# Feed-forwards' last matrices: the last pair of tiles keeps its seven operands on chip and goes second

## The chip, the cores and the metric

The kernel runs on one core of a Trainium2 chip. The core has a matrix engine (TensorE, PE in the profile), a vector engine (VectorE, DVE), an activation engine (ScalarE, ACT), GpSimd (POOL), and an engine that issues most of the transfers (SyncE, SP). Data lies in HBM, in the on-chip buffer SBUF, and in PSUM, into which TensorE writes its products. SP, ACT and POOL can each start transfers (DMAs); the queue of SP is called SPq in the profile, that of ACT is ACTq. Each engine works through its own list in the order written there, so an instruction that waits holds up everything behind it on that engine.

The metric is the time of one execution on the device in microseconds (us). The kernel before takes 2007.23 us, the median of three runs (2004.85 to 2007.33).

## The reference

One layer of a streaming encoder on 1,040 tokens (16 meta tokens and 1,024 frames) of width 1,024:

```python
h = h + 0.5 * swiglu(rmsnorm(h, ffn1_norm), ffn1_w_gate, ffn1_w_up, ffn1_w_down)
u = rmsnorm(h, mix_norm)
...                                   # window attention and gated linear attention on u @ w_in
h = h + mixed @ w_out
h = h + 0.5 * swiglu(rmsnorm(h, ffn2_norm), ffn2_w_gate, ffn2_w_up, ffn2_w_down)
return rmsnorm(h, final_norm)[:, N_META:]

def swiglu(x, w_gate, w_up, w_down):
    return (silu(x @ w_gate) * (x @ w_up)) @ w_down
```

The change concerns the two feed-forwards (`ffn1`, `ffn2`). The inner width is 2,816, which is 22 tiles of 128 columns. All of it is 32-bit: each factor of a product is split into a high and a low part, and three products of the parts are added.

## The kernel before, in words

**A feed-forward in two halves.** The class `Seven` holds one feed-forward. In the first half, `gate_up(f)` makes one tile f of the inner activations, silu(gate) times up, transposed: 128 inner columns by all tokens, as two halves m0 and m1 of the tokens (520 tokens each in the first feed-forward, 512 in the second). In the second half, `down`, the inner activations are multiplied with `w_down` and added to h.

**Seven products instead of eight.** Both halves use a 2 by 2 block scheme with seven products (`PRODUCTS`), each a sum of a weight block times a sum of activation blocks. The seven right-hand operands are called B11, B21, T2, T1, T3, B22 and T4. For `down` they are made from a pair of tiles, f = 2p and 2p + 1. `middle(f, m0, m1)` collects two tiles and appends seven little pieces of work to the list `pending`; `pump` does the next of them whenever it is called, which is seven times in each `gate_up` and at seven slots at the beginning of `down`. Such a piece subtracts blocks where the operand is a difference (VectorE, L277) and then calls `keep`: high part by ScalarE (L237), low part by VectorE (L238), two transfers into a tensor `mid` in HBM (L240, L241).

**The second half.** `down` runs over five groups of two pairs (`NG` = 5), each group in two steps, one for each half of the output columns, so ten steps of seven slots. A slot is one of the seven products: 24 matmuls of 260 columns in the first feed-forward, 12 of 512 in the second. In slot i TensorE multiplies the weight operand `w` (made two slots ahead by ScalarE L228 and VectorE L229, the tiles `wop`) with the operand `tm` of both pairs. The 14 operand tiles of the first group are loaded by SP before the first slot. Those of the next groups are loaded through ACT's own queue, one per slot, in the order in which they are needed (`load_t`, L347). When a slot's sum is complete it goes from PSUM to h: the first time by ScalarE (L396), afterwards by VectorE (`add_half`, L341). GpSimd makes the four sums of weight blocks for the next step (L437). From the second step on the old h is read back (`old`, L408) and added (L404).

**The last pair.** The pair of tiles 18 and 19 is finished when `down` begins. Its seven pieces of work, in `down`'s first slots, use four small buffers (`ttile`), and their transfers go through GpSimd, since `ending` is set. The pair is loaded again with its partner as the fifth and last group.

**The two tiles outside the groups.** 22 tiles are five groups of four and two left over (`LAST` = 2, tiles 20 and 21). These go to `w_down` as plain products at the very end (`load_last`), and their high and low parts are kept in `last_dram`. Some tiles are computed before the scheme starts, as plain products. In the first feed-forward these are tiles 20 and 21 (`HEADS`) and tile 0; in the second they are tiles 0 and 1 (`heads`), and tiles 2 to 21 run through `gate_ups`.

**What sets the order.** A scheduler orders each engine's instructions from the program's text, its data and its buffers. An operand buffer `tm` comes from one of two rings: eight buffers for B11 and B21 and twenty for the others, which is what two groups need. During the first half the same buffers hold the activation operands (`tt`, `tb`).

## Time and profile before

| | us |
|---|---|
| median of three runs | 2007.23 |
| the profiled execution | 2007.16 |
| span in its profile | 2005.5 |
| TensorE busy in the span | 1979.6 |
| VectorE, ScalarE, GpSimd busy | 1406.9, 895.9, 178.5 |
| first feed-forward's `down`, from its first product | 480.10 on |
| second feed-forward's `down`, from its first product | 1772.68 on |

The span goes from the first to the last instruction that the profiler recorded. Times within it are in us from its start. A row of the timeline of one engine gives start, duration, engine, line, operation and how many like it follow each other; in square brackets it gives the idle time just before, and what ended it. A row of busy time by stretches gives the stretch, its length, then busy time and number of instructions of PE, PEld (weight loads), DVE, ACT and POOL, then the granted clock of TensorE as a share of full speed, the busy share of the 16 DMA engines and GB/s. A row of transfers gives what is written from what, the queue, the count, the size in KB of 1,024 bytes and the median time in us from issue to landing.

### The profile page before, as it was taken

To read this page: it belongs to the slowest core of one execution; us is meant where nothing else is said; L and a number is where in the kernel's file an instruction comes from. 1 tells how busy PE (TensorE), PEld (TensorE's weight loads), DVE (VectorE), ACT (ScalarE), POOL (GpSimd) and SP (SyncE) were. 2 spreads that over 40 slices of the span, in tenths; PEclk is the share of its full clock that TensorE was granted. 3 is DMA by queue.
4 is the path that set the end of the run, shared out by engine and by line. 5 is a ranking of instruction groups with operands and counts; after the bars stand their busy time and mean duration, and the time that the engine had idled before them with its cause. 6 is when DMAs were issued, how large, how long until landed. Compare 5 with 4: busy or idle time off the path is not lost.

```text
span 2005.5 us, 31822 instructions
## 1 busy us (share of the span) xinstructions
PE 1979.6 (99%) x11964; PEld 1756.2 (88%) x11964; DVE 1406.9 (70%) x2455; ACT 895.9 (45%) x1756; POOL 178.5 (9%) x214
## 2 busy tenths in 40 slices
PE   8999999999999999999999999999999999999998
PEld 7999999999999988888888878888888888878887
DVE  6976776676778786476466568469767767757786
ACT  5544444443322254465366545345444444442225
POOL 1000000002323000004100000110000000022220
PEclk9999999999999999999999999999999999999999
DMA  6243453349975333356212647741534534699832
GB/s 212 86 149 128 149 180 129 125 147 378 363 278 199 96 128 106 117 178 180 53 54 69 213 146 224 238 148 47 189 126 148 189 126 140 206 362 346 299 106 85
DMA packets 284619, 343.03 MB, mean 171 GB/s; under 512 B 26407, under 2 KB 192033, under 8 KB 284465
## 3 DMA queue, kind: packets, MB, share of 16 engines
q1 hardware_dynamic: 265376, 274.82, 41.6%
q10 hardware_dynamic: 17296, 61.29, 8.1%
q0 software_dynamic: 1792, 4.89, 0.7%
q8 instruction: 94, 1.54, 0.3%
q14 instruction: 61, 0.49, 0.1%
HBM read 220.66 MB, written 120.27 MB: 170 GB/s over the span
## 4 chain that ended last, share of the span: by engine, by line
PE 92%; DVE 3%; DMA 2%; issue 1%; ACT 1%; POOL 0%; SPq 0%; POOLq 0%; ACTq 0%; DVEq 0%
PE pb L454 36%; PE pd L454 18%; PE pa L454 9%; PE pj L96 2%; PE pj L97 2%; PE pj L98 2%; PE wo L96 1%; PE wo L98 1%; PE wo L97 1%; PE br L96 1%; PE br L98 1%; PE br L97 1%; PE pd L841 1%; PE pj L929 1%; PE pj L930 1%
## 5 line engine op out<-in xcount | busy, mean ns | idle before, releaser
L454 PE MATMUL pb<-tt,wop 128*128 128x260 f32 (+1 forms) x2280 | 393.0, 326 | 0.0
L454 PEld LDWEIGHTS pb<-tt,wop 128*128 128x128 f32 x2280 | 339.7, 188 | 35.5
L228 ACT CAST wop<-s 128x512 fp32r<-128x512 f32 x268 | 166.1, 621 | 235.4 <-PE pb L454 97.4
L229 DVE TENSOR_TENSOR wop<-s,wop 128x512 fp32r<-128x512 f32 x268 | 188.8, 707 | 116.2 <-ACT wop L228 115.7
L454 PE MATMUL pb<-tm,wop 128*128 128x260 f32 (+1 forms) x1440 | 236.4, 320 | 8.0 <-DMA tm<-f2mid 3.5
L454 PEld LDWEIGHTS pb<-tm,wop 128*128 128x128 f32 x1440 | 208.2, 189 | 28.5 <-ACT h L396 2.8
L228 ACT CAST wop<-raw 128x512 fp32r<-128x512 f32 x201 | 124.9, 622 | 221.8 <-PE pb L454 113.2
L229 DVE TENSOR_TENSOR wop<-raw,wop 128x512 fp32r<-128x512 f32 x201 | 144.0, 718 | 30.9 <-ACT wop L228 30.7
L454 PE MATMUL pd<-tt,wop 128*128 128x260 f32 (+1 forms) x792 | 138.2, 327 | 0.0
L454 PEld LDWEIGHTS pd<-tt,wop 128*128 128x128 f32 x792 | 118.8, 188 | 13.1
L341 DVE SCALAR_TENSOR_TENSOR h<-pb,h 128x520 f32<-128x520 f32 (+1 forms) x136 | 93.9, 692 | 39.7 <-PE pb L454 37.7
L454 PE MATMUL pd<-tm,wop 128*128 128x260 f32 (+1 forms) x720 | 118.8, 319 | 0.0
L454 PE MATMUL pb<-tb,wop 128*128 128x260 f32 (+1 forms) x696 | 115.3, 319 | 0.7 <-DVE m L742 0.7
L454 PE MATMUL pd<-tb,wop 128*128 128x260 f32 (+1 forms) x696 | 115.1, 319 | 0.0
L454 PE MATMUL pa<-tb,wop 128*128 128x260 f32 (+1 forms) x696 | 115.0, 318 | 0.0
L454 PEld LDWEIGHTS pd<-tm,wop 128*128 128x128 f32 x720 | 104.3, 188 | 9.3
L454 PEld LDWEIGHTS pb<-tb,wop 128*128 128x128 f32 x696 | 100.9, 188 | 10.1 <-ACT vec L87 0.8
L454 PEld LDWEIGHTS pa<-tb,wop 128*128 128x128 f32 x696 | 100.7, 188 | 9.4
L454 PEld LDWEIGHTS pd<-tb,wop 128*128 128x128 f32 x696 | 100.7, 188 | 9.4
L437 DVE TENSOR_TENSOR s<-raw 128x512 f32<-128x512 f32 x92 | 63.2, 687 | 56.1 <-DMA raw<-in_ffn_w_up 52.8
L96 PE MATMUL pj<-uh,whi 128*128 128x512 f32 (+2 forms) x256 | 91.5, 357 | 0.0
L437 POOL TENSOR_TENSOR s<-raw 128x512 f32<-128x512 f32 x28 | 37.8, 1351 | 595.4 <-DMA raw<-in_ffn_w_down 472.5
(418 smaller groups left out, 3888.0 us busy)
## 6 DMA issues: line engine op xcount, KB each, us to landing
tm<-f1mid ACTq DMA_DIRECT2D x56, 520.0 KB, 6.3
tm<-f2mid ACTq DMA_DIRECT2D x56, 512.0 KB, 5.7
raw<-in_ffn_w_gate SPq DMA_DIRECT2D x42, 512.0 KB, 3.9
raw<-in_ffn_w_up SPq DMA_DIRECT2D x42, 512.0 KB, 4.0
raw<-in_ffn_w_down SPq DMA_DIRECT2D x80, 256.0 KB, 5.3
f2mid<-kh SPq DMA_DIRECT2D x70, 256.0 KB, 2.9
f2mid<-kl SPq DMA_DIRECT2D x70, 256.0 KB, 3.1
f1mid<-kh SPq DMA_DIRECT2D x63, 260.0 KB, 2.7
```

Source lines behind the costliest of these rows:

```text
L96: nc.tensor.matmul(ps, wh[k], xh[k], start=(k == 0), stop=False)
L97: nc.tensor.matmul(ps, wh[k], xl[k], start=False, stop=False)
L98: nc.tensor.matmul(ps, wl[k], xh[k], start=False, stop=(k == n - 1))
L228: nc.scalar.copy(x[:, 0:n], src)
L229: nc.vector.tensor_sub(x[:, n:2 * n], src, x[:, 0:n].bitcast(F32))
L341: nc.vector.scalar_tensor_tensor(hm, ps, 0.5, hm, op0=ALU.mult, op1=ALU.add)
L437: (eng.tensor_add if add else eng.tensor_sub)(a[s], a[x], a[y])
L454: nc.tensor.matmul(ps, y, z[:, s0:s0 + sn], start=(first and k == 0 and at == 0), stop=(at == 2 and k == len(cols) - 1), skip_group_check= ...
L841: nc.tensor.matmul(ps, y, x[:, c0 + s0:c0 + s0 + sn], start=(n == 0), stop=(n == 3 * LAST - 1), skip_group_check=True)
L929: nc.tensor.matmul(ps[:, 0:n], wh, xh, start=(k == 0), stop=False)
L930: nc.tensor.matmul(ps[:, 0:n], wh, xl, start=False, stop=False)
```

## The change

The last pair's operands are no longer written to HBM and read back. `middle` sends the pieces of pair 18, 19 to `halves`, which writes high and low part into an operand buffer `tm` (`down_tile`) that `down` then uses in place. Since these buffers are held until used, the group with this pair goes second: `ORDER` is [0, 4, 1, 2, 3]. The second group loads only its first pair, seven tiles; `load_t` skips the other seven. The branch in `keep` for the end (`ttile`, GpSimd) is gone.

So that the last pair is the last thing that `gate_ups` makes in the second feed-forward too, its plain tiles are now the last two, as in the first: `heads` uses `HEADS` (tiles 20 and 21), and `gate_ups` runs over tiles 0 to 19. Their four `keep`s into `last_dram` happen at the start of the first half instead of at the end.

```diff
+    ORDER = [0, NG - 1, *range(1, NG - 1)]
...
         def keep(self, dst, src):
-            hi, lo = [ttile(x, F32R, self.n) if self.ending else self.block(x, F32R) for x in ("kh", "kl")]
+            hi, lo = [self.block(x, F32R) for x in ("kh", "kl")]
             nc.scalar.copy(hi, src)
             nc.vector.tensor_sub(lo, src, hi.bitcast(F32))
-            eng = nc.gpsimd if self.ending else nc.sync
-            eng.dma_start(out=dst[:, 0:self.n], in_=hi.bitcast(F32))
-            eng.dma_start(out=dst[:, self.n:], in_=lo.bitcast(F32))
+            nc.sync.dma_start(out=dst[:, 0:self.n], in_=hi.bitcast(F32))
+            nc.sync.dma_start(out=dst[:, self.n:], in_=lo.bitcast(F32))
...
-                    self.keep(d[NAMES.index(n)], src)
+                    if f == NF - LAST - 1:
+                        self.here[n] = self.halves(self.down_tile(n), src)
+                    else:
+                        self.keep(d[NAMES.index(n)], src)
...
-        def load_t(self, kg, ts, at, eng):
+        def down_tile(self, n):
+            return self.operand(n in ("B11", "B21"), "tm")
 
-            n, a = NAMES[at // 2], at % 2
-            x = self.operand(n in ("B11", "B21"), "tm")
-            eng.dma_start(out=x.bitcast(F32), in_=self.mid_dram[2 * kg + a, NAMES.index(n)])
-            ts.setdefault(n, []).append(x)
+        def load_t(self, turn, at, eng):
+
+            n, pair = NAMES[at // 2], 2 * ORDER[turn] + at % 2
+            if pair < 2 * NG - 1:
+                x = self.down_tile(n)
+                eng.dma_start(out=x.bitcast(F32), in_=self.mid_dram[pair, NAMES.index(n)])
+                self.ts.setdefault((turn, n), []).append(x)
...
-            kg, half = step // 2, step % 2
+            kg, half = ORDER[step // 2], step % 2
...
-                    pss = [group.product(i, w, ts[step // 2], (j * P, 2 * P + j * P), j, step) for j in range(2)]
+                    ts = {NAMES[i]: self.ts[step // 2, NAMES[i]]}
+                    if step // 2 == 1:
+                        ts[NAMES[i]] = ts[NAMES[i]][0:1] + [self.here[NAMES[i]]]
+                    pss = [group.product(i, w, ts, (j * P, 2 * P + j * P), j, step) for j in range(2)]
...
-    heads = [[ffn2.plain_weights(cols_view(w, f * P)) for w in (ffn2_w_gate, ffn2_w_up)] for f in range(2)]
+    heads = [[ffn2.plain_weights(cols_view(w, f * P)) for w in (ffn2_w_gate, ffn2_w_up)] for f in HEADS]
...
-    for f in range(2):
-        ffn2.middle(f, *out_c[f])
-    ffn2.gate_ups(range(2, NF))
+    for f in range(LAST):
+        ffn2.middle(HEADS[f], *out_c[f])
+    ffn2.gate_ups(range(NF - LAST))
```

The list of TensorE is the same before and after, row for row. The lists of the others differ at the start of both `down`s and at the start of the second feed-forward's first half. Names in the rows: `h` is the output, `wop` a weight operand, `raw` and `s` the weights and their sums, `tm` an operand of `down`, `kh` the high part that `keep` makes. In brackets stand the semaphores that a row waits for: DMAHW0 to DMAHW7 are eight completion semaphores which all transfers of SP and ACT use in turn, DMASW0 to DMASW7 those of GpSimd's transfers. A transfer that takes its turn on DMAHW2 is issued only when the one that used DMAHW2 before it has landed.

ACT, at the beginning of the first feed-forward's `down`, before: four of the second group's loads stand earlier still in the list, and three more stand here between the moves of the first sums from PSUM to h.

```order
L237 CAST kh<-g_5681 128x520 [waits DMASW1_49,DMASW2_49,DMASW0_49,DMASW3_49,DVE_49,Activation_49]
L396 ACTIVATE h_5951<-pb 128x520 [waits PE_49]
L396 ACTIVATE h_5953<-pb 128x520 [waits PE_49]
L228 CAST wop<-raw_5871 128x512 [waits DMAHW7_49]
L347 DMA tm<-f1mid 128x1040 [waits DMAHW4_49]
L347 DMA tm<-f1mid 128x1040 [waits DMAHW6_49]
L228 CAST wop<-raw 128x512 [waits DMAHW0_49,PE_49,Activation_49]
L396 ACTIVATE h_6027<-pb 128x520 [waits PE_49]
L347 DMA tm<-f1mid 128x1040 [waits DMAHW2_49]
L396 ACTIVATE h_6029<-pb 128x520 [waits PE_49]
L396 ACTIVATE h_6067<-pd 128x520 [waits DMAHW0_49,PE_49]
L237 CAST kh<-tm 128x520 [waits DMASW5_49,DVE_49]
```

The same place now:

```order
L229 CAST tm<-g_5681 128x520 [waits DVE_49,Activation_49]
L354 DMA tm<-f1mid 128x1040 [waits DMAHW2_49]
L406 ACTIVATE h_5951<-pb 128x520 [waits PE_49]
L406 ACTIVATE h_5953<-pb 128x520 [waits PE_49]
L229 CAST wop<-raw_5871 128x512 [waits DMAHW3_49]
L354 DMA tm<-f1mid 128x1040 [waits DMAHW5_49]
L229 CAST wop<-raw 128x512 [waits DMAHW4_49,PE_49,Activation_49]
L406 ACTIVATE h_6021<-pb 128x520 [waits PE_49]
L406 ACTIVATE h_6023<-pb 128x520 [waits PE_49]
L229 CAST wop<-raw 128x512 [waits Activation_49]
L229 CAST tm<-tm 128x520 [waits DVE_49]
L406 ACTIVATE h_6058<-pd 128x520 [waits DMAHW4_49,PE_49]
```

The first load of the second group now stands just ahead of the first move to h; none stands between `h_6021` and `h_6023`, the rows that were `h_6027` and `h_6029`. The pieces of the last pair wait for no transfer any more.

ACT, at the beginning of the second feed-forward's `down`, before:

```order
L228 CAST wop<-raw_18333 128x512 [waits DMAHW4_49]
L347 DMA tm<-f2mid 128x1024 [waits DMAHW7_49]
L347 DMA tm<-f2mid 128x1024 [waits DMAHW1_49]
L317 COPY u_18209<-pd 128x512 [waits PE_49]
L228 CAST wop<-s 128x512 [waits Activation_49]
L347 DMA tm<-f2mid 128x1024 [waits DMAHW4_49]
L228 CAST wop<-s 128x512 [waits PE_49,Activation_49]
L347 DMA tm<-f2mid 128x1024 [waits DMAHW7_49]
L228 CAST wop<-s 128x512 [waits PE_49,Activation_49]
L324 ACTIVATE g_18264<-g_18264 128x512 [waits DVE_49]
L228 CAST wop<-s 128x512 [waits PE_49,Activation_49]
```

and now:

```order
L321 COPY u_18150<-pd 128x512 [waits PE_49,Activation_49]
L229 CAST wop<-s 128x512 [waits Activation_49]
L229 CAST wop<-s 128x512 [waits PE_49,Activation_49] x2
L328 ACTIVATE g_18193<-g_18193 128x512 [waits DVE_49]
L229 CAST wop<-s 128x512 [waits PE_49,Activation_49]
L229 CAST tm<-g_18149 128x512 [waits DVE_49]
L354 DMA tm<-f2mid 128x1024 [waits DMAHW6_49,DMAHW4_49]
L406 ACTIVATE h_18335<-pb 128x512 [waits PE_49]
```

The four loads of the second group that stood inside the last `gate_up` are gone from there; the first one follows behind the last `gate_up`'s work.

SP, at the beginning of the first feed-forward's first half, now:

```order
L666 DMA f1last<-kept 128x1040 [waits DMAHW6_49,DVE_49]
L666 DMA f1last<-kept 128x1040 [waits DMAHW7_49,DVE_49]
L418 DMA old<-x_dram 128x520 [waits DMAHW0_49,DVE_49,Activation_49]
L418 DMA old<-x_dram 128x520 [waits DVE_49,DMAHW1_49,Activation_49,Pool_49]
L418 DMA old<-x_dram 128x520 [waits DMASW2_49,DMASW3_49,DMASW1_49,DMAHW2_49,DMASW0_49,PE_49]
L418 DMA old<-x_dram 128x520 [waits DMAHW3_49,DVE_49,Pool_49]
L298 DMA raw<-in_ffn_w_gate 128x8x128 [waits DMAHW4_49,DVE_49]
L298 DMA raw<-in_ffn_w_up 128x8x128 [waits DMAHW5_49,DVE_49]
```

and before:

```order
L656 DMA f1last<-kept 128x1040 [waits DMAHW6_49,DVE_49]
L656 DMA f1last<-kept 128x1040 [waits DMAHW7_49,DVE_49]
L294 DMA raw<-in_ffn_w_gate 128x8x128 [waits DMAHW4_49,DMAHW0_49,DVE_49]
L294 DMA raw<-in_ffn_w_up 128x8x128 [waits DMAHW5_49,DMAHW1_49,DVE_49]
L294 DMA raw<-in_ffn_w_gate 128x8x128 [waits DMAHW0_49,DMAHW2_49,DVE_49,Activation_49]
```

The four `ttile` buffers are no longer used at the end of the first half, so the scheduler has moved the first four reads of the old h to its beginning, ahead of the next weights. In the second feed-forward four such reads stand at the same place.

## The prediction

> **What bounds the kernel now.** I read the page's busy times first, then what TensorE waits for.

> ```profile
> span 2005.5 us, 31822 instructions
> PE 1979.6 (99%) x11964; PEld 1756.2 (88%) x11964; DVE 1406.9 (70%) x2455; ACT 895.9 (45%) x1756; POOL 178.5 (9%) x214
> ```

> ```profile
> PE pb L454 <- DMA tm<-f2mid: 3.5, 2, 2.0
> PE pb L454 <- ACT h L396: 2.6, 1, 2.6
> ...
> PE pb L454 <- DVE h L341: 1.9, 2, 1.3
> ```

> TensorE is idle for 25.9 us in all, and its list of work is the same after the change. So only its gaps can be won. The three rows are all it waits for at L454, 8.0 us, and all lies in the first slots of the two `down`s, where the change acts. I measure what these places cost from start to start of the same product in successive steps, since a stall may also slow what follows. TensorE's timeline, first feed-forward, then the second (`pa` is product 1 of a step):

> ```profile
> 482.96 3.03 PE L454 MATMUL pa<-tm,wop 128*128 128x260 f32 x24
> ...
> 495.85 1.70 PE L454 MATMUL pb<-tm,wop 128*128 128x260 f32 x12 [2.61 <-ACT h L396]
> ...
> 504.58 1.70 PE L454 MATMUL pb<-tm,wop 128*128 128x260 f32 x12 [1.28 <-DVE h L341]
> 506.87 1.71 PE L454 MATMUL pb<-tm,wop 128*128 128x260 f32 x12 [0.60 <-DVE h L341]
> 508.42 3.03 PE L454 MATMUL pa<-tm,wop 128*128 128x260 f32 x24
> ...
> 528.57 1.59 PE L454 MATMUL pa<-tm,wop 128*128 128x260 f32 x12
> ```

> ```profile
> 1775.40 2.88 PE L454 MATMUL pa<-tm,wop 128*128 128x512 f32 x12
> ...
> 1786.28 2.88 PE L454 MATMUL pd<-tm,wop 128*128 128x512 f32 x12
> 1790.68 0.94 PE L454 MATMUL pb<-tm,wop 128*128 128x512 f32 x3 [1.51 <-DMA tm<-f2mid]
> 1793.60 6.69 PE L454 MATMUL pb<-tm,wop 128*128 128x512 f32 x21 [1.98 <-DMA tm<-f2mid]
> 1800.13 2.88 PE L454 MATMUL pa<-tm,wop 128*128 128x512 f32 x12
> ...
> 1819.17 2.88 PE L454 MATMUL pa<-tm,wop 128*128 128x512 f32 x12
> ```

> First feed-forward: the first step takes 508.42 - 482.96 = 25.46 us, the second 528.57 - 508.42 = 20.15. The first loses **5.31 us**, of which 4.49 are gaps. Second: 1800.13 - 1775.40 = 24.73 against 1819.17 - 1800.13 = 19.04, so **5.69 us**, of which only 3.49 are gaps. Most of the rest is in the row of 21 matmuls: 6.69 us, where 12 take 2.72 from start to start (1800.13 is 2.72 before the next product), so 21 should take 4.8. The stretches behind the stall show why:

> ```profile
> 1794.00:1797.00 3.00, 3.00 (x10) 2.32 (x9) 0.51 (x1) 0.00 (x0) 0.00 (x0) 0.58 1.04 384
> 1797.00:1800.00 3.00, 3.00 (x13) 2.41 (x12) 0.00 (x0) 0.16 (x1) 0.88 (x1) 0.85 0.88 302
> 1800.00:1803.00 3.00, 3.00 (x15) 2.49 (x14) 1.50 (x3) 2.93 (x6) 2.92 (x3) 1.00 1.04 303
> ```

> The granted clock falls to 0.58 and 0.85, and at full clock 15 matmuls start where 10 and 13 did. That is 6.69 - 4.8 = 1.9 us which the stall costs beyond its gaps.

> **The change part by part.** *What makes the first stall.* ACT's and VectorE's timelines:

> ```profile
> 494.82 0.33 ACTq L347 DMA_DIRECT2D tm<-f1mid  x1
> 495.19 0.60 ACT L396 ACTIVATE h<-pb 128x520 f32<-128x520 f32 x1 [7.12 <-DMA tm<-f1mid]
> ```

> ```profile
> 503.21 0.70 DVE L238 TENSOR_TENSOR kl<-u,kh 128x520 fp32r<-128x520 f32 x1 [2.32 <-DMA f1mid<-kl]
> ...
> 505.51 0.70 DVE L238 TENSOR_TENSOR kl<-u,kh 128x520 fp32r<-128x520 f32 x1 [0.99 <-DMA f1mid<-kl]
> ```

> ACT could not issue a load of the second group until an earlier transfer had landed; behind it in ACT's list waited the move of a sum to h, and behind that TensorE's next product into the same PSUM (495.85). Then VectorE waited for the small buffers of `keep` to be written out; behind it waited further moves to h (504.58, 506.87). The change removes both: no load stands between these moves any more, and the last pair has no transfer. Term: **-5.31 us**.

> *What makes the second stall.* Operands of the first group arrive late. SP's last ten loads, ACT's first two, and the last of the ten in the chain of waits:

> ```profile
> 1763.08 15.22 SPq L347 DMA_DIRECT2D tm<-f2mid  x10
> ```

> ```profile
> 1762.11 0.81 ACTq L347 DMA_DIRECT2D tm<-f2mid  x2
> ```

> ```profile
> 1777.98 15.58 DMA tm<-f2mid
> ```

> The last load is issued at 1777.98 and lands at 1793.56. Without any stall its first matmul would run 2.72 us (product 5 to 6) and three matmuls of 0.23 after 1786.28, at 1789.7. It must land 3.9 us sooner. The transfers at 1770 to 1795, the sizes and the queues:

> ```profile
> DMA packets 3799, 10.16 MB, mean 407 GB/s; under 512 B 390, under 2 KB 1579, under 8 KB 3797
> ...
> tm<-f2mid ACTq DMA_DIRECT2D x4, 512.0 KB, 7.8
> ...
> f2last<-kh POOLq DMA_DIRECT2D x2, 256.0 KB, 8.7
> ```

> All DMA engines are full and give 0.407 MB per us. What leaves the way of the first group: the eight `f2last` transfers of 0.262 MB (two tiles by two token halves, high and low part; four of them on SP, ahead of these loads, four on GpSimd), 2.1 MB, and the four loads of ACT inside the last `gate_up`, 4 x 0.524 = 2.1 MB. Two of these four vanish with the last pair; the others come later. 4.2 MB at 0.407 are 10.3 us, against 3.9 needed. The first reads of the old h leave this place too. Term: **-5.69 us**. If only part of it comes sooner, a landing still 1 us late costs 1 us.

> *The second group.* Seven loads instead of 14, used from the fifteenth slot on: nothing, and there is nothing to gain, since TensorE waits for nothing there now.

> *What is added.* Seven copies by ScalarE and eleven instructions of VectorE (seven low parts, four differences) in slots 0 to 8 of each `down`. The first feed-forward has them already, as `keep`. In the second, `keep` ran twice, so five copies of some 0.6 us (as ScalarE's row at 495.19) and nine VectorE instructions are new there (the four differences and five low parts). Duration, undisturbed and while GpSimd makes its sums:

> ```profile
> 1758.03 0.69 DVE L238 TENSOR_TENSOR kl<-g,kh 128x512 fp32r<-128x512 f32 x1 [1.49 <-ACT kh L237]
> ...
> 1774.72 1.78 DVE L238 TENSOR_TENSOR kl<-g,kh 128x512 fp32r<-128x512 f32 x1
> ```

> ```profile
> 1772.95 1.30 POOL L437 TENSOR_TENSOR s<-raw 128x512 f32<-128x512 f32 x1 [425.64 <-DMA raw<-in_ffn_w_down]
> ...
> 1777.60 1.74 POOL L437 TENSOR_TENSOR s<-raw,s 128x512 f32<-128x512 f32 x1
> ```

> Slots 0 to 8 last 9 x 2.72 = 24.5 us. VectorE has 9 weight operands, 8 moves to h and these 11 there, 28 x 0.69 = 19.3 us. During GpSimd's four sums, 1772.95 to 1779.34, it does 6.39 / 1.78 = 3.6 instructions where 9.3 would fit, which adds 5.7 x 0.69 = 3.9. That is 23.2 of 24.5 us: hidden, narrowly. Upper bound: GpSimd's next four sums fall into the same slots, 3.9 more, 27.1, which is 2.6 us too much. Nothing can be won here. I take **+0.3 us**, near the lower end, since the first feed-forward does the same work in 25.9 us of slots and stalls on transfers alone, and keep 0 and 2.6.

> *What is moved.* The four `keep`s of the plain tiles go to the start of the second feed-forward, where seven pieces stood; there, near 1400 us, the transfers are far from full (slices 28 and 29 of the page's 40, 47 and 189 GB/s). Nothing.

> ```profile
> GB/s 212 86 149 128 149 180 129 125 147 378 363 278 199 96 128 106 117 178 180 53 54 69 213 146 224 238 148 47 189 126 148 189 126 140 206 362 346 299 106 85
> ```

> The four early reads of the old h stand on SP ahead of the next weights; bounds are under the rivals. I take 0.

> *The sum.* The profiled execution took 2007.16 us, 1.66 more than its span, and agrees with the median of 2007.23. 2007.16 - 5.31 - 5.69 + 0.3 = **1996.5 us**, 0.53% faster.

> **The rivals.** *VectorE becomes the bound.* The sums of GpSimd and the eleven instructions meet, and moves to h come late, as at 504.58. For it: 23.2 of 24.5 us. Against: what the first feed-forward shows. [...] Price: gaps of 1 to 2.6 us, and up to 1.9 for the clock behind them: 1998 to 2001.

> *The low clock stays.* If it had another cause than the gaps, 1.9 us remain: 1998.4. Against: it begins right behind them. [...]

> *The stall only moves.* ACT's loads still wait, in ACT's list, for an earlier transfer to land; the first now stands ahead of the first move to h. If landings are as late as now (15.58 us), ACT is held as at 495.19, and one stall comes back: 1996.5 + 5.3 = 2001.8, or both: 2007. Against: that first load waits for the landing of operands that TensorE needs one slot later anyway, and 4.2 MB are out of the way.

> *Slower: SP is held by the early reads of the old h.* One of the four waits for the buffer that a transposition on TensorE reads, and the weights stand behind it:

> ```profile
> L86 PE MATMUL vps<-ident,vrow x2: 234/252/271, 4.9 to 96.8; 8*128 8x8 f32 x1, 19*128 19x19 f32 x1
> ```

> ```profile
> 100.77 0.38 SPq L294 DMA_DIRECT2D raw<-in_ffn_w_gate  x1
> 103.78 0.38 SPq L294 DMA_DIRECT2D raw<-in_ffn_w_up  x1
> ```

> ```profile
> 115.22 5.75 PE pb L454 x48
> ```

> ```profile
> raw<-in_ffn_w_up SPq DMA_DIRECT2D x42, 512.0 KB, 4.0
> ```

> The weights go out at 100.77 and 103.78 now, and their `gate_up` begins at 118.1 (half of the last row); with 4.0 us of landing and five VectorE instructions of 0.69 (three sums, an operand, one in the way) the slack is 118.1 - 103.8 - 4.0 - 3.4 = 7 us. If a buffer came free only when the running `gate_up` ends, 20.1 us later, each feed-forward would lose 20.1 - 7 = 13 us: 1996.5 + 26 = 2022. It decides when SP is held past about 108 us. Against: as I read the buffers' last uses, that transposition at 96.8 is the latest work that the waits in the list name.

> **How the numbers follow.** Both stalls go: 0.68, 1995 to 1998. The low clock stays: 0.03, 1998.4. VectorE becomes the bound: 0.13, 1998 to 2001. A stall stays or moves: 0.12, 2001.5 to 2007. SP is held: 0.04, above 2007. The range of 1994.5 to 2001.5 leaves out the last two and reaches 2 us below the sum, because runs differ by 2.5 us. A measurement tells 0.2%, 4 us, from no change: faster means below 2003.2. From the third case a third lies there: 0.68 + 0.03 + 0.13 + 0.04 = 0.88; same 0.08; slower 0.04.

> **What would show it.** Right: in TensorE's waits no row for L454 with `tm<-f2mid`, `h L396` or `h L341` above 0.5 us; `pa` to `pa` 20.1 and 19.0 us in the first step too; a granted clock of 1.00 throughout 1770 to 1800; the first group's last load landed before its slot; TensorE's busy time lower by 5.31 + 5.69 - 4.49 - 3.49 = 3 us, the part of the two losses that was no gap. Wrong: a new row for L454 released by VectorE (second case), by ACT or a transfer (third), or a gap at L454 in the first `gate_up`s near 118 or 1410 (fourth).

## The result, and the profile after

The changed kernel takes **1996.19 us** (median of four runs, 1995.26 to 1997.96), the kernel before 2007.28 us beside it (2004.85 to 2009.59). The ratio is 0.9947 with a 95% interval of 0.9933 to 0.9961: 10.6 us less by the ratio (7.8 to 13.4), 11.1 by the medians. The forecast was 1996.5 us and 10.7 us less. The profiled execution took 1996.54 us. The first lines of its page:

```profile
span 1994.6 us, 31746 instructions
PE 1976.3 (99%) x11964; PEld 1755.8 (88%) x11964; DVE 1402.4 (70%) x2455; ACT 897.2 (45%) x1756; POOL 166.9 (8%) x196
```

The span is 10.9 us shorter. TensorE's busy time fell from 1979.6 to 1976.3, its idle time from 25.9 to 18.3: 3.3 us and 7.6 us. The changed kernel's waits of TensorE begin with these rows (in total, times, longest); line 464 is what was line 454.

```profile
PE xps L567 <- DMA x<-in_x: 2.8, 1, 2.8
...
PE pb L464 <- DVE m L752: 0.7, 1, 0.7
```

The only wait left at the products is the 0.7 us at the start of the first half, which stood there before. `tm<-f2mid`, `h L396` and `h L341` are gone. TensorE's timeline where the two `down`s begin:

```profile
482.61 3.03 PE L464 MATMUL pa<-tm,wop 128*128 128x260 f32 x24
...
497.03 5.90 PE L464 MATMUL pb<-tm,wop 128*128 128x260 f32 x48
502.76 3.03 PE L464 MATMUL pa<-tm,wop 128*128 128x260 f32 x24
```

```profile
1770.32 2.88 PE L464 MATMUL pa<-tm,wop 128*128 128x512 f32 x12
...
1789.36 2.88 PE L464 MATMUL pa<-tm,wop 128*128 128x512 f32 x12
```

From `pa` to `pa` the first steps now take 502.76 - 482.61 = 20.15 us and 1789.36 - 1770.32 = 19.04 us, like the steps behind them, where they took 25.46 and 24.73. That is 5.31 + 5.69 = 11.0 us, where the span fell by 10.9 and the profiled execution by 10.6. Outside these two steps the two profiled executions nearly agree: the changed kernel's is 0.35 us shorter ahead of the first `down`, 0.58 longer between the end of that `down`'s first step and the beginning of the second `down`, and 0.13 shorter behind. The stretches in which the clock had been low (columns as before: length, busy time of PE, PEld, DVE, ACT, POOL, granted clock, share of the DMA engines, GB/s):

```profile
1776.00:1779.00 3.00, 3.00 (x15) 2.49 (x14) 1.70 (x4) 3.00 (x7) 0.00 (x0) 1.00 0.55 175
...
1794.00:1797.00 3.00, 3.00 (x15) 2.49 (x14) 0.69 (x1) 1.94 (x4) 0.00 (x0) 1.00 0.83 280
```

The clock is 1.00 throughout, and from 1776 on the DMA engines are no longer full. The operands of the first group, in the rows on SP's loads of `tm` from 1740 to 1800 (instructions, first and last start; then the shortest, median and longest time to landing):

```profile
L354 SPq DMA_DIRECT2D tm<-f2mid x14: 319/351/1217, 1749.4 to 1764.7; - x14
DMA to landing us min/median/max: 4.1/8.4/10.2
```

The last load goes out at 1764.7 and has landed by 1774.9, which is 7.3 us after the `down`'s first product (1767.60). Before, it landed 1793.56 - 1772.68 = 20.9 us after it, with 17.0 allowed. In the first `down`, ACT issues its second load of the second group at 482.82 and the next one only at 491.52:

```profile
482.82 0.33 ACTq L354 DMA_DIRECT2D tm<-f1mid  x1
...
491.52 0.33 ACTq L354 DMA_DIRECT2D tm<-f1mid  x1
```

In between it makes three moves to h, none of them late. Before, one load stood among them and went out at 494.82, and the move behind it had waited 7.12 us.

### The profile page after: what moved, and what is told of

It is laid out like the page before. It is cut to its first block, busy times and chain, and to the rows that moved or that the text cites. A ratio compares the mean times of both kernels' runs of the same rounds, so it can differ in the third digit from the quotient of the medians.

```text
span 1994.6 us, 31746 instructions
## 1 busy us (share of the span) xinstructions
PE 1976.3 (99%) x11964; PEld 1755.8 (88%) x11964; DVE 1402.4 (70%) x2455; ACT 897.2 (45%) x1756; POOL 166.9 (8%) x196
## 5 line engine op out<-in xcount | busy, mean ns | idle before, releaser
L230 DVE TENSOR_TENSOR wop<-raw,wop 128x512 fp32r<-128x512 f32 x201 | 140.0, 697 | 34.3 <-ACT wop L229 34.2
L464 PEld LDWEIGHTS pb<-tb,wop 128*128 128x128 f32 x696 | 100.9, 188 | 10.2 <-ACT vec L87 0.8
## 6 DMA issues: line engine op xcount, KB each, us to landing
tm<-f2mid ACTq DMA_DIRECT2D x49, 512.0 KB, 4.6
raw<-in_ffn_w_gate SPq DMA_DIRECT2D x42, 512.0 KB, 3.9
raw<-in_ffn_w_up SPq DMA_DIRECT2D x42, 512.0 KB, 3.9
raw<-in_ffn_w_down SPq DMA_DIRECT2D x80, 256.0 KB, 5.1
f2mid<-kh SPq DMA_DIRECT2D x63, 256.0 KB, 2.8
```

The source lines that it names most:

```text
L230: nc.vector.tensor_sub(x[:, n:2 * n], src, x[:, 0:n].bitcast(F32))
L464: nc.tensor.matmul(ps, y, z[:, s0:s0 + sn], start=(first and k == 0 and at == 0), stop=(at == 2 and k == len(cols) - 1), skip_group_check= ...
```

## The experiments

The theory to be tested: each feed-forward has a stall of its own. In the first, ACT's list is held by a load of the second group, and then VectorE's by the small buffers; in the second, too many transfers stand ahead of the first group's. The rivals: the two are one thing, or another part of the change does the work. All kernels are compared with the kernel before, which took 2006.93, 2007.2 and 2005.87 us in the first three batches (medians), and 2007.64 beside the last run. "Less" is by the ratio, with its interval. Lost time is again counted from `pa` to `pa` against 20.15 and 19.04 us.

### One feed-forward at a time

A table says which feed-forward keeps the last pair on chip; the other does as before. For the first alone the second also keeps its old order of tiles.

```diff
+    LOCAL = {'f1': True, 'f2': False}
...
-                    if f == NF - LAST - 1:
+                    if self.local and f == NF - LAST - 1:
```

> The change in the first feed-forward alone; the second as before. Theory (two separate stalls, one in each feed-forward): 2007.2 - 5.3 = 2001.9 us; in the first down the first step takes 20.15 us from pa to pa and TensorE's waits lose the rows for h L396 and h L341; in the second the first step stays at 24.7 us with 3.5 us of waiting for operands from f2mid and a granted clock near 0.6 behind it. Rival (one saving depends on the other, for example through the transfers of the whole kernel): 2007 or 1996.

Measured: 2000.37 us (six runs), ratio 0.9972 (0.9960 to 0.9984), 5.6 us less (3.2 to 8.0). Its second `down`:

```profile
1769.51 2.88 PE L469 MATMUL pa<-tm,wop 128*128 128x512 f32 x12
...
1784.07 0.93 PE L469 MATMUL pb<-tm,wop 128*128 128x512 f32 x3 [0.80 <-DMA tm<-f2mid]
1786.40 6.43 PE L469 MATMUL pb<-tm,wop 128*128 128x512 f32 x21 [1.41 <-DMA tm<-f2mid]
1792.67 2.88 PE L469 MATMUL pa<-tm,wop 128*128 128x512 f32 x12
```

The first `down` loses nothing. The second still waits for `f2mid`, now 23.16 - 19.04 = 4.12 us in place of 5.69. The stall is the same, its size is not fixed.

> The change in the second feed-forward alone; the first as before. Theory: 2007.2 - 5.7 + 0.3 = 2001.8 us; the second down's first step takes 19.04 us with a granted clock of 1.00, the first down keeps 25.4 us with the gaps of 2.6, 1.3 and 0.6 us. Rival (the savings are not separate): outside 2000 to 2003.5.

The table with the two words exchanged, and the plain tiles last. Measured: 2003.67 us (eleven runs), ratio 0.9985 (0.9976 to 0.9994), 3.0 us less (1.2 to 4.8) where 5.4 were expected. The second `down` loses nothing (19.04). The first:

```profile
481.67 3.03 PE L469 MATMUL pa<-tm,wop 128*128 128x260 f32 x24
...
495.08 2.97 PE L469 MATMUL pb<-tm,wop 128*128 128x260 f32 x12 [3.14 <-ACT h L411]
...
507.98 3.03 PE L469 MATMUL pa<-tm,wop 128*128 128x260 f32 x24
```

```profile
498.00:501.00 3.00, 3.00 (x17) 3.00 (x16) 2.12 (x4) 0.09 (x1) 2.21 (x3) 0.54 1.02 374
```

Here it loses 26.31 - 20.15 = 6.16 us: ACT's gap is 3.14 instead of 2.61, and the clock falls to 0.54 behind it, which it had not done in the first feed-forward of the kernel before. The two later gaps for VectorE's moves are absent; this one gap and the half clock behind it, about 3 us each, are the whole loss. So the two savings are separate in place, and each stall vanishes where its part is changed, but what is left of the other differs by 1 or 2 us from execution to execution. The 2003.67 us lie just above the 2000 to 2003.5 that were expected of separate savings, and the interval, about 2002.0 to 2005.6, does not decide there; 5.6 + 3.0 = 8.6 agrees with the 10.6 of both within the intervals.

### Only the order of the second feed-forward's tiles

The changed kernel with both words of the table off, so that both last pairs go through HBM as before. What is left of the change is the order of the second feed-forward's tiles:

```diff
-    heads = [[ffn2.plain_weights(cols_view(w, f * P)) for w in (ffn2_w_gate, ffn2_w_up)] for f in range(2)]
+    heads = [[ffn2.plain_weights(cols_view(w, f * P)) for w in (ffn2_w_gate, ffn2_w_up)] for f in HEADS]
...
-    for f in range(2):
-        ffn2.middle(f, *out_c[f])
-    ffn2.gate_ups(range(2, NF))
+    for f in range(LAST):
+        ffn2.middle(HEADS[f], *out_c[f])
+    ffn2.gate_ups(range(NF - LAST))
```

> Only the order of the second feed-forward's tiles: its plain tiles are the last two, all operands go through HBM as before. The second down then has what the first has: 2.1 MB fewer transfers at its end, but seven pieces with small buffers and GpSimd's transfers in its slots, and ACT's loads between the moves. Theory: the wait for f2mid goes (2.1 MB at 0.407 MB per us are 5.2 us, 3.9 are needed), and a stall like the first feed-forward's 5.3 us comes in its place, with waits for h L396 and h L341: 2007.2 - 5.7 + 5.3 = 2006.8 us. Rival (the order of the tiles alone cures the second stall): 2001.5 us, and no new wait for h.

Measured: 2008.12 us, ratio 1.0007 (0.9998 to 1.0016). The wait for `f2mid` is gone, as 2.1 MB less ahead of it would have it, and the first feed-forward's stall has come to the second. TensorE's timeline there, and ACT's:

```profile
1789.37 2.93 PE L469 MATMUL pb<-tm,wop 128*128 128x512 f32 x6 [2.56 <-ACT h L411]
...
1804.63 3.02 PE L469 MATMUL pb<-tm,wop 128*128 128x512 f32 x12 [1.30 <-ACT h L411]
```

```profile
1788.29 0.33 ACTq L358 DMA_DIRECT2D tm<-f2mid  x1
1788.72 0.60 ACT L411 ACTIVATE h<-pb 128x512 f32<-128x512 f32 x1 [6.72 <-DMA tm<-f2mid]
...
1801.94 0.62 ACT L241 CAST kh<-g 128x512 fp32r<-128x512 f32 x1 [2.97 <-DMA f2mid<-kh]
```

The first gap is the pattern of 495.19 in the kernel before: ACT's next load cannot go out until an earlier transfer has landed, and the move to h stands behind it. The second comes from the small buffers: ACT's next high part (`kh`) waits until one of them has been written out, and a move to h stands behind that. (In the second feed-forward of the kernel before, the last pair's pieces ran in the `gate_up` of tile 20, and only two pieces of tile 21 lay in `down`'s slots; with the plain tiles last the pair's pieces lie in the slots there too.) The second `down` loses 4.29 us in its first step and 1.59 in its second, 5.9 us for the 5.69 it had. The order of the tiles is worth nothing without the operands on chip.

### The second group's loads on SP's queue

The kernel before, with the loads of one group taken out of ACT's list and nothing else:

```diff
-                        self.load_t(kg, ts[kg], at, nc.scalar)
+                        self.load_t(kg, ts[kg], at, nc.sync if kg == 1 else nc.scalar)
```

> The kernel before, with the loads of the second group on SP's queue and not on ACT's; the small buffers and GpSimd's transfers stay. Theory (ACT's list held by its load makes the first gap; the small buffers make the next two): in the first down the gap of 2.6 us for h L396 goes, the gaps for h L341 (1.9 us together) stay, so some 3 us of its 5.3 go; in the second, ACT's four early transfers (2.1 MB, 5.2 us) go behind the first group's, 3.9 us are needed, so all 5.7 go: 2007.2 - 3 - 5.7 = 1998.5 us. Rival (ACT was only late because all transfers were): the gap of 2.6 us stays, 2002 to 2007. Other rival (SP is now held by these loads, and the weights behind them come late): new waits at L454 for wop, above 2007.

Measured: 2002.56 us, ratio 0.9982 (0.9973 to 0.9991), 3.6 us less (1.8 to 5.4) where 8.7 were expected. TensorE's timeline in the first `down`:

```profile
498.74 1.71 PE L454 MATMUL pb<-tm,wop 128*128 128x260 f32 x12 [0.66 <-DVE h L341]
502.07 3.15 PE L454 MATMUL pb<-tm,wop 128*128 128x260 f32 x24 [1.62 <-DVE h L341]
505.05 3.03 PE L454 MATMUL pa<-tm,wop 128*128 128x260 f32 x24
...
514.39 3.15 PE L454 MATMUL pb<-tm,wop 128*128 128x260 f32 x24 [0.48 <-ACT h L396]
...
528.43 4.67 PE L454 MATMUL pa<-tm,wop 128*128 128x260 f32 x24 [1.98 <-ACT h L396]
...
550.19 3.03 PE L454 MATMUL pa<-tm,wop 128*128 128x260 f32 x24
```

In the first step ACT's gap is gone and VectorE's two stay, 2.28 us of gaps where 1.9 were: the two causes are separate, as the prediction had them. In the second `down` nothing is lost. ACT's early loads alone out of the way are therefore enough there, as the `f2last` transfers alone were in the run before. What was not expected are the next two steps of the first `down`: 528.43 - 505.05 = 23.38 us, 3.23 too long, and 550.19 - 528.43 = 21.76 us, 1.61 too long: the 24 matmuls behind the gap of 1.98 take 4.67 us, where those of the next step take 3.03. ACT's timeline shows why the gaps come:

```profile
513.36 0.33 ACTq L347 DMA_DIRECT2D tm<-f1mid  x1
513.73 1.10 ACT L396 ACTIVATE h<-pb 128x520 f32<-128x520 f32 x2 [4.99 <-DMA tm<-f1mid]
...
527.35 0.33 ACTq L347 DMA_DIRECT2D tm<-f1mid  x1
527.78 1.10 ACT L396 ACTIVATE h<-pb 128x520 f32<-128x520 f32 x2 [2.99 <-DMA old<-x_dram]
```

The third group's loads now do to ACT what the second group's did: one holds it for 4.99 us, which costs TensorE 0.48, and a later one, held until a read of the old h has landed, for 2.99 us, which costs 1.98 and the 1.61 behind it. The three steps lose 2.83 + 3.23 + 1.61 = 7.7 us in the first feed-forward, which had lost 5.31. The hold of ACT has moved by one group, and all of the gain comes from the second feed-forward: 5.31 + 5.69 - 7.67 = 3.3, in agreement with the measured 3.6.

### Transfers put back

The changed kernel, with four more `keep`s of tile 18 (`keep_twice`, its text and its tensor not shown) in the second feed-forward's last `gate_up`, each written twice, into a tensor that nothing reads (in the second kernel six of them):

```diff
+            if f == NF - LAST - 2 and self.name == "f2":
+                for i in range(4):
+                    self.pending.append(lambda i=i: self.keep_twice(self.more_dram[i // 2, i % 2], self.more_dram[4 + i // 2, i % 2], (m0, m1)[i % 2]))
...
```

> The changed kernel with 4.2 MB of transfers put back: in the last gate_up of the second feed-forward SP writes sixteen more pieces of 0.262 MB (four keeps of tile 18, each written twice, into a tensor that nothing reads), ahead of the last twelve loads of the first group. In the changed kernel the last of these loads is issued at 1764.7 and lands 10.2 us later at the latest, 1774.9, which is 7.3 us after the second down's start (1767.6); the operand is needed 17.0 us after it (the seventh slot and three matmuls). Theory (transfers ahead of the first group make the stall, 0.407 MB per us): landing 10.3 us later, 17.6 after the start: a stall of 0 to 1.5 us, 1996.2 to 1998. Rival (the amount of transfers was not the cause, but that ACT's loads and SP's shared the queues): 1996.2, landing near 7 after the start.

Measured: 1999.16 us, ratio 0.9964 (0.9952 to 0.9975), 3.0 us over the changed kernel's median. The waits are there, but earlier than expected:

```profile
1772.74 1.60 PE L476 MATMUL pb<-tm,wop 128*128 128x512 f32 x6 [0.47 <-DMA tm<-f2mid]
1775.24 1.67 PE L476 MATMUL pb<-tm,wop 128*128 128x512 f32 x6 [0.89 <-DMA tm<-f2mid]
1777.62 1.66 PE L476 MATMUL pd<-tm,wop 128*128 128x512 f32 x6 [0.71 <-DMA tm<-f2mid]
```

The third and fourth products wait, and the last load, which the expectation looked at, decides nothing: no product waits after these. The extra pieces stand on SP ahead of the loads of the second operand and all behind it, and the third operand is due 5.4 us after the first product, not 17. The cost follows from the first operand that is late. A transfer takes no longer to land than in the changed kernel (at most 10.3 us, 10.2 there), but the last one goes out at 1778.1 instead of 1764.7: here the lateness lies in when SP comes to issue, where in the kernel before the landing was longer too (15.58). The time is 1.2 us above the 1998 up to which the theory was to hold.

> As the run with 4.2 MB put back, but with 6.3 MB (24 pieces). Theory: landing 15.5 us later than in the changed kernel, 22.8 us after the second down's start, where 17.0 are allowed: a stall of 5.8 us for f2mid, and with the low clock behind it up to 1.9 more: 2002 to 2004. Rival (amount not the cause): 1996.2 and no wait for f2mid.

Measured: 2007.3 us (ten runs, 2004.31 to 2009.9), ratio 1.0003 (0.9993 to 1.0012): 6.3 MB put back take away all that the change gave, more than the 6 to 8 us expected. The profiled execution took 2004.31, the fastest of the ten. There the second `down` lost 8.0 us from its first product to the next step: 5.6 in gaps, the longest 3.76 ahead of the second product, and behind that a clock of 0.59 from 1776 to 1779. The last load goes out at 1781.6 there and landings take 10.2 us at most. In both runs the amount and the place in SP's list act together, and the extra pieces are also work for ACT and VectorE; that transfers ahead of the first group make a stall of this kind is shown, the price of a megabyte is not.

### More work for VectorE

The changed kernel with each of the seven low parts computed twice, and in the second kernel, which the diff shows, three times:

```diff
-                        self.here[n] = self.halves(self.down_tile(n), src)
+                        x = self.here[n] = self.halves(self.down_tile(n), src)
+                        for _ in range(2):
+                            nc.vector.tensor_sub(x[:, self.n:2 * self.n], src, x[:, 0:self.n].bitcast(F32))
```

> The changed kernel, with each of the seven low parts of the last pair's operands computed twice by VectorE: seven instructions of 0.69 us more in slots 0 to 8 of each down, 4.8 us. By the prediction's count (23.2 of 24.5 us taken in the second feed-forward) VectorE would be 3.5 us over there: a stall of some 3.5 us in the second feed-forward at least, 1999.7 to 2003. Rival: the changed kernel's trace has VectorE busy for 17.7 us in 1767 to 1791 only, because GpSimd's first four sums now stand before the down, so 4.8 more fit: 1996.2, no new wait at the products.

Measured: 1996.8 us, ratio 0.9955 (0.9940 to 0.9969), no wait at the products. The 4.8 us fit.

> The changed kernel, with each of the seven low parts of the last pair computed three times: 14 instructions of 0.69 us more, 9.7 us in each down. With seven more VectorE was busy for 26.2 of the 27 us from 1770 to 1797 and TensorE lost nothing. Theory (VectorE is the next bound there, and seven were just within it): 4 us too much in the second feed-forward, 2 in the first, as waits at the products for h or wop released by VectorE: 1998 to 2003. Rival (the instructions can still spread over later slots): 1996.2 to 1997.2, no new wait.

Measured: 1997.53 us, ratio 0.9958 (0.9944 to 0.9972), and one new wait of 0.3 us. With 9.7 us more in each `down`, VectorE is busy almost without a break from 1782 to 1791:

```profile
1785.00:1788.00 3.00, 3.00 (x15) 2.48 (x14) 3.00 (x5) 1.52 (x3) 0.99 (x1) 1.00 0.68 194
```

and TensorE, in the first column behind the comma, loses nothing there. These low parts are used from the fifteenth slot on, not in slots 0 to 8, and VectorE does the moves to h in between. The rival expectation holds: the work spreads over later slots.

### The last pair's group as the last one

```diff
-    ORDER = [0, NG - 1, *range(1, NG - 1)]
+    ORDER = [0, 1, 2, 3, 4]
...
-                    if step // 2 == 1:
+                    if ORDER[step // 2] == NG - 1:
```

> The changed kernel with the group of the last pair as the last one (order 0, 1, 2, 3, 4), its seven operands held on chip until then, so that 21 buffers of 28 are left for the groups before it. Theory (the gain comes from what no longer stands in ACT's and VectorE's lists and in the queues at the start of down; the place in the order only sets how early the loads can start): a load can start when its buffer comes free, seven slots or 19 us ahead of its use, and landings take 5 us: 1996.2 to 1998. Rival (the place second is what makes it work): ACT's list is held by loads that wait for buffers, with moves to h behind them, 2 to 5 us in each feed-forward: 2000 to 2006.

Measured: 1997.51 us, ratio 0.9961 (0.9948 to 0.9974), which overlaps the changed kernel's interval. No wait at the products, 20.15 and 19.04 us in the first steps. With 21 buffers the other groups' loads still come in time. The second group has 14 loads in ACT's list again, and no move to h is late for TensorE. So neither the pair's place nor the total number of the second group's loads gives the gain. What did not change is the first step: in both kernels ACT issues the same six loads in it, 1.0, 3.1, 11.8, 14.7, 17.6 and 18.9 us after the first product (479.75 and 482.11), where the kernel before had issued four ahead of the first product, from 465.91 on. The number of loads in the first step was not varied by itself.

### Gaps made on purpose

What remained was the low clock: in the kernel before it followed the gap of 1.98 us in the second `down` (0.58 from 1794 to 1797) and not that of 2.61 in the first (1.00 from 495 to 501). In the changed kernel GpSimd rewrites the low part of one weight operand several times in some steps, so that TensorE waits for it far from any full transfers:

```diff
+                    if step > 1 and i == 3:
+                        for _ in range(4 + (step - 2) % 4):
+                            nc.gpsimd.tensor_sub(w[:, WB:], group.a[PRODUCTS[i][1]], w[:, 0:WB].bitcast(F32))
```

> The changed kernel with gaps made on purpose in TensorE's work, with no lack of transfers: in steps 3 to 10 of each down GpSimd computes the low part of the fourth product's weight operand four, five, six or seven times over (1.3 to 1.8 us each), so that TensorE waits for it once per step, for 0 to 6 us. Looked at is the granted clock behind each gap. Theory (the gaps make the low clock): stretches of about 3.4 us at a low clock behind some of the gaps, with transfers far from full; gaps under 1.5 us have none. [...] Rival that the low clock came from the full transfers: 1.00 behind all gaps.

It made no gap at all (1999.8 us, one run): the chains of 6.1 to 10.5 us on GpSimd were over before the operand was needed. Longer chains, in every second step (`step in (2, 4, 6, 8)`, 8, 8, 9 and 10 times):

> As the run with gaps on purpose, which made none: there the operand was made 11.4 us ahead of its product, and chains of 6 to 10 us on GpSimd were over before it. Now eight, eight, nine and ten times over, in steps 3, 5, 7 and 9 of each down: chains of 13 to 17 us with GpSimd's own sum among them, gaps of about 2 to 5 us, transfers far from full. Theory (the gaps make the low clock): a stretch of about 3.4 us at a low clock behind some gaps. [...] Rival (full transfers made it): 1.00 throughout.

2028.7 us (one run) and a gap at seven of the eight chains. TensorE's timeline in both `down`s, the row behind each gap, two rows behind one of them, and three of the stretches that follow (the first matmuls of the product, which use the high part alone, run ahead of the gap):

```profile
530.87 2.65 PE L467 MATMUL pd<-tm,wop 128*128 128x260 f32 x20 [1.73 <-POOL wop L400]
573.66 2.68 PE L467 MATMUL pd<-tm,wop 128*128 128x260 f32 x20 [2.31 <-POOL wop L400]
617.82 4.03 PE L467 MATMUL pd<-tm,wop 128*128 128x260 f32 x20 [3.63 <-POOL wop L400]
664.12 4.70 PE L467 MATMUL pd<-tm,wop 128*128 128x260 f32 x20 [4.42 <-POOL wop L400]
1833.30 4.63 PE L467 MATMUL pd<-tm,wop 128*128 128x512 f32 x10 [2.84 <-POOL wop L400]
1837.73 3.73 PE L467 MATMUL pb<-tm,wop 128*128 128x512 f32 x12
1841.30 2.89 PE L467 MATMUL pd<-tm,wop 128*128 128x512 f32 x12
1915.43 2.56 PE L467 MATMUL pd<-tm,wop 128*128 128x512 f32 x10 [2.73 <-POOL wop L400]
1959.30 3.97 PE L467 MATMUL pd<-tm,wop 128*128 128x512 f32 x10 [5.13 <-POOL wop L400]
```

```profile
618.00:621.00 3.00, 3.00 (x15) 3.00 (x16) 0.70 (x1) 0.00 (x0) 2.35 (x2) 0.52 0.00 0
1833.00:1836.00 3.00, 2.71 (x6) 2.15 (x7) 3.00 (x4) 0.00 (x0) 2.92 (x3) 0.50 1.01 393
1915.00:1918.00 3.00, 2.57 (x11) 2.16 (x12) 0.69 (x1) 0.00 (x0) 2.91 (x3) 1.00 0.14 56
```

Twenty matmuls take 2.65 us behind the gap of 1.73 and 4.70 behind that of 4.42. The gaps of 1.73, 2.31 and 2.73 us are followed by full clock (1.00 in the 3 us from 531, 574 and 1915), those of 2.84, 3.63, 4.42 and 5.13 by half (0.50, 0.52, 0.50 and 0.50 in the 3 us from 1833, 618, 664 and 1959). At 618 no transfer runs and the clock is 0.52, so full transfers are not needed for it. Nor does the length alone decide: behind 2.73 it is 1.00 here and behind 2.61 in the kernel before, where behind 2.56 in the run with only the tiles reordered, and behind 0.80 + 1.41 in the run with the first feed-forward alone, it is 0.68 and 0.65. The last section sets the gaps against the times at which the half clock begins.

## Why the prediction was right, point by point

*What bounds the kernel, and the two losses.* Right, and to the hundredth in the profiled execution: both first steps took exactly what the later ones take, 5.31 and 5.69 us less. Busy time was to fall by 3 us and fell by 3.3. The exactness is partly luck. The stalls' sizes vary (the first 5.31, 6.16 and 6.45 us in the three traces that have it unchanged, the second 5.69 and 4.12), the sum was made from one execution that agreed with the median, the small differences outside the two steps nearly cancel, and the 0.3 us that the sum had added for VectorE did not come.

*What makes the first stall.* Right, and the hold of ACT's list is shown: the run with SP's queue took away ACT's gap and left VectorE's two, and the run with the tiles reordered made the same hold of ACT in the second feed-forward, 6.72 us where the first had 7.12. The part of the small buffers rests on what the traces give as the releaser (`f1mid<-kl`, 2.32 us, in the kernel before, `f2mid<-kh`, 2.97, in the reordered one); no run takes the small buffers alone away. The prediction's "no load stands between these moves any more" is what the changed kernel's ACT list shows; where the second group's loads were put elsewhere with the small buffers still in use, the third's held ACT in their place.

*What makes the second stall.* The mechanism was right, the size of one step was not. The last load was to land 10.3 us sooner (4.2 MB at 0.407); against the first product it landed at least 13.6 us sooner (20.9 to 7.3). It went out 8.2 us sooner already: 1778.0 was 5.3 us after the first product, 1764.7 is 2.9 ahead of it. The rest is a shorter way to landing, 10.2 at most for 15.58. Since 3.9 were needed, nothing came of it. The two shares of 2.1 MB were each enough: with either gone (the reordered tiles, and ACT's early loads in the run with SP's queue) no wait for `f2mid` was left.

*VectorE.* The term of +0.3 was in effect 0, and the working behind it was wrong: "23.2 of 24.5 us: hidden, narrowly" set the end of slot 8 as the deadline of work that is due from the fifteenth slot on, and put GpSimd's first four sums into those slots. They stand at 1761.60 to 1771.02 now, and only the last, from 1769.33 on, lies wholly in the `down`, which begins at 1767.60. Before, the first of them, at 1772.95, was released by the DMA of the weights; now VectorE releases it. 9.7 us more fitted. The rival that VectorE becomes the bound had little ground at 0.13.

*What is moved.* Nothing, as forecast. The plain tiles' transfers and the order of the groups cost nothing that the traces show. The four early reads of the old h are held up on SP until the transposition, and the weights behind them are not late, in SP's timeline of the changed kernel. The next two loads of weights go out at 100.42 and 103.43 (100.77 and 103.78 before):

```profile
86.29 11.35 SPq L418 DMA_DIRECT2D old<-x_dram  x4
```

The last of the four ends at 97.64, just behind the transposition at 96.44, as the reading of the waits had it.

*The rivals.* "The low clock stays" fell in the profile after: 1.00 throughout. "The stall only moves" did not happen here, but did in the run with SP's queue. Its mechanism was real. What keeps it away in the changed kernel is not the total number of the second group's loads, since with the group last there are 14 again. In the first step the loads begin later, and the last pair's own transfers are gone, and no run separates these two.

No kernel that was run beats the changed one; the three whose intervals lie on its own (group last, more work for VectorE) do the same work or more.

## What to carry to other kernels

A transfer that an engine issues between its own instructions can hold them all until an earlier transfer has landed (here ACT for 7.12, 6.72 and 4.99 us): look in the trace for that engine's idle time released by a DMA, and for what stands behind the issue in its list. Taking such loads out of one place only helps if the next ones behind them are not held in the same way (with the second group's loads on SP's queue the first feed-forward lost 7.7 us instead of 5.31). When transfers are late, price the stall by the first operand that is due, and put a deadline on added work by where its result is first used, not by where it is written.

## What was not expected of the hardware

The half clock came behind one gap and not behind another of nearly the same length: behind 2.84 us and not behind 2.73 in the run with gaps made on purpose. These are stretches of 1 us around its four spells of half clock (length, busy time of PE, granted clock, share of the DMA engines, GB/s):

```profile
617.00:618.00 1.00, 0.18 (x1) 0.74 0.00 0
661.00:662.00 1.00, 0.00 (x0) 0.93 0.01 4
1832.00:1833.00 1.00, 0.00 (x0) 0.81 1.05 416
1958.00:1959.00 1.00, 0.00 (x0) 0.96 0.00 0
```

In the 3.41 us just ahead of the four beginnings TensorE was idle for 3.29, 2.16, 2.16 and 3.41 us, by the rows shown above. The other three gaps can be placed by an estimate alone: if stretches of 3.41 us are counted on from these beginnings, 1.73 lies in one, 2.31 is cut into 1.76 and 0.55, and 2.73 into 1.85 and 0.88. By that estimate 2.16 us of idle time in 3.41 were followed by the half clock in this run, and 1.85 were not; that such stretches govern the clock is not shown.

The same count for other traces, each from its own clock. In the second `down` of the kernel before the clock is 0.75 from 1794 to 1795, 0.50 up to 1797 and 0.54 up to 1798: half from 1794.50 to 1797.92, 3.42 us, and the 3.41 us ahead of it hold the whole gap of 1.98. With the tiles reordered it is 0.68 from 1788 and 0.75 from 1791: half from 1789.1 to 1792.5, and the 3.41 us ahead hold about 2.3 of the gap of 2.56. In the run with the first feed-forward alone it is 0.65 from 1785 and 0.78 from 1788: half from 1785.9 to 1789.3, and the 3.41 us ahead hold about 1.7 of the 0.80 + 1.41. So about 1.7 us went ahead of the half clock there, where by the estimate 1.85 in the run on purpose did not: no limit on the idle time is shown. In other places of the kernel, with smaller matmuls, the half clock also followed a shorter gap (1.25 us up to 22.00 in the kernel before; the clock is 0.50 from 23 to 26), so the gaps in the rows are not the whole measure.

A gap of 2.84 us on purpose cost more in clock than in waiting: its 10 matmuls and the 12 behind them took 8.00 us from 1833.30 to 1841.30, where 22 take 5.0 (2.72 for 12): 3.0 us more.
